# The raw weights' third buffer in the first trunk, and two re-ordered steps of the normalised operands

## The chip, the cores and the metric

The kernel runs on one core of a Trainium2 chip. The metric is the device time of one execution in microseconds (us). The core has five engines with queues of their own: TensorE (PE in the profile, with PEld for its weight loads), VectorE (DVE), ScalarE (ACT), GpSimd (POOL) and SyncE (SP). SyncE computes nothing here; it issues DMA transfers. GpSimd issues some as well.

## The reference

One layer of an encoder is applied to 1024 prompt rows and 32 sample rows (`x`), which share the weights; the model width is 1024. Cut to what is computed:

```python
h = rms_norm(x, g_mix)
q, k, v, ch, cb, cc, ga, gb = split(h @ w_in)            # 1024 x 6656
a = window_attention(q, k, v, sink) @ w_attn_out
conv = short_convolution(cc * ch, conv_w)                # width 3, causal
bo = (cb * conv) @ w_conv_out
x = x + (sigmoid(ga) * a + sigmoid(gb) * bo) @ w_mix_out
hc = rms_norm(x, g_cross)
x = x + softmax_attention(hc @ w_cq, mem_k, mem_v) @ w_co  # 256 memory tokens
hm = rms_norm(x, g_mlp)
x = x + square(relu(hm @ w_up)) @ w_down                 # 1024 -> 4096 -> 1024
y = rms_norm(x, g_final)
```

New rows of the K/V and convolution caches are outputs too. All is float32.

## The kernel before

**Layout.** Activations are held transposed: 128 features on the partitions, tokens along the free axis. The 1056 tokens are cut into three chunks `CH` of 384, 384 and 288 columns (chunks 0, 1, 2) for the first part of the layer, and into two halves for the MLP. `f` counts the eight blocks of 128 features. Each float32 operand is split into a high and a low part in TensorE's `fp32r` form, and each product is three matmuls: high by high, high by low, low by high (`gemm`, L193 to L195; `product`, L864 to L866, in the gates and the up projection; L1770 to L1772 in the down projection).

**Weights.** A weight tile of 128 x 1024 floats (512 KB) is loaded raw by SyncE (`fetch_w`, L155), then split: `wh` by an ACT cast (L129), `wl` by a DVE subtraction (L130). `next_w` keeps two split weights in stock ahead of the one in use. A raw tile is one of the two `wr` buffers of pool `wp`. While the dictionary `third` is filled, every third raw tile instead comes from the pool `third["pool"]`, under the tag `ws` (the trace calls it `wr` as well, the order `wr3`). For the keys in `kept` the low part is stored once into `wl_d` (L172) and loaded in later uses (L166) instead of being subtracted again.

**GpSimd's sums.** The MLP's products use sums of weight blocks. `sum_step` (L702 to L725) makes them on GpSimd, one piece after another: it loads raw blocks into a tile, `ws` of pool `W["pool"]` and `xacc` by turns, adds (L719), and stores the sums into `gsum_d`, `usum_d` or `wsum_d` by GpSimd's own queue (L723). One `ws` tile is all that pool has.

**Stages, in the order of the plan.** Keys and values; attention; the gates (`gate_pair`), which use a third raw buffer from a pool of theirs; then `after_gates`, which gives `third` the pool `W["pool"]` from then on. Then come the *trunks*: for each chunk eight `do_conv_out` (L1042) and eight `do_mix` (L1057). Chunk 0's trunk, with one conv_out of chunk 1 put in, runs first; chunk 1's runs beside cross attention of chunk 0; chunk 2's is made into *fillers*, 48 items together with the first up projections. After filler `i` the steps that `then(i, ...)` names are called: statistics, cross attention, and `normed(c, f)` (L1277), which makes block `f` of chunk `c` of the MLP's normalised operand: a DVE multiplication (L1279), a store into `xn_d` by SyncE (L1282), and for chunk 0 an ACT cast and a DVE subtraction (L1291). The first half's operand is made straight from chunk 0. The second half's (tiles `Z` of `xa[1]`) starts in chunk 0 and ends in chunk 1: `open_first` loads its first part back from `xn_d` (L1229) after filler 18, and `normed` of chunk 1 copies the rest from the tile `ct` (L1284). Both are SyncE's transfers. `ct` tiles come from a pool of six (`tmp`).

**What sets the order.** The plan's items are recorded in program order; a scheduler then orders each engine's instructions by its own estimate of when they can run. Instructions given to `pin` keep their place in program order relative to one another. An instruction whose semaphore is not yet reached holds all that stands behind it on its engine's queue, SyncE's transfers included.

Of the kernel before, what the change touches and what calls it, by code (L numbers as in the profile page):

```python
# [10 lines left out]
F32 = mybir.dt.float32  # L11
# [11 lines left out]
CH = [(0, 384), (384, 384), (768, 288)]  # L23
NF = 8
HT = 528
QT = 264
# [14 lines left out]
def hybrid_step(ctx: ExitStack, tc: tile.TileContext, io):  # L41
    nc = tc.nc
    act, dve, pool_e, pe, sp = nc.scalar, nc.vector, nc.gpsimd, nc.tensor, nc.sync
# [3 lines left out]
    def nm(s):  # L47
        uid[0] += 1
        return f"{s}_{uid[0]}"

    def opened(name, **kw):
        cm = tc.tile_pool(name=name, **kw)
        return cm, cm.__enter__()

    def closed(cm):
        cm.__exit__(None, None, None)
# [17 lines left out]
    def col(j):  # L74
        return prm[:, j : j + 1]
# [6 lines left out]
    xn_d = dram.tile([P, NF, NT], F32, name="xn_d")  # L82
# [14 lines left out]
    def pin(ins):  # L97
        return tc.keep_in_program_order(ins)
# [6 lines left out]
    def tmp(n, dt=F32):  # L105
        return tp.tile([P, n], dt, tag="ct", bufs=NCT, name=nm("ct"))
# [9 lines left out]
    plan, worder, kept = [], [], {}  # L116

    def item(fn, *keys):
        plan.append((fn, keys))
        worder.extend(keys)  # L120
# [11 lines left out]
    def weight(key):  # L132
        name, *at = key
        if name in ("w_down", "w_sum"):
            q, j, t = at
            return (wsum_d if name == "w_sum" else io[name])[j, t, :, :, q].rearrange("i p c -> p i c")
        if name == "g_sum":
            return gsum_d[at[0]][:, at[1]].rearrange("p h c -> p (h c)")
        src = io[name]
        for j in at:  # L140
            src = src[j]
        return src

    fetched = []
    third = {}

    def fetch_w():
        if third:
            third["n"] += 1
        if third and third["n"] % 3 == 0:  # L150
            raw = third["pool"].tile([P, 4, 256], F32, tag="ws", name=nm("wr3")).rearrange("p q c -> p (q c)")
        else:
            raw = wp.tile([P, 1024], F32, tag="wr", bufs=2, name=nm("wr"))
        src = weight(worder[wpos[0] + len(fetched)])
        sp.dma_start(raw.rearrange("p (i c) -> p i c", i=4) if len(src.shape) == 3 else raw, src)  # L155
        fetched.append(raw)

    def issue_w():
# [55 lines left out]
    def xacc_tile():  # L214
        xacc[0] = tp.tile([P, 1056], F32, tag="xacc", name=nm("xacc"))
        return xacc[0]
# [59 lines left out]
    W = {}  # L276
# [458 lines left out]
    for i, h in enumerate(hosts):  # L735
        kv, p = i // 8, i % 8
# [30 lines left out]
    def yslot(c):  # L767
        return slot(Y[c if c < 2 else "top"], f"Y{c}", CH[c][1])
# [22 lines left out]
    def pump(n):  # L791
        for into, at, t, get in coming:
            hi, lo = into[at] = (get(), get())
            pin(act.copy(hi, t))
            pin(dve.tensor_sub(lo, t, hi.bitcast(F32)))
        coming.clear()
        for into, at, src, cols, get in wanted[:n]:
            t = cols() if callable(cols) else tmp(cols)
            sp.dma_start(t, src)
            coming.append((into, at, t, get))  # L800
        del wanted[:n]
# [216 lines left out]
    def after_gates():  # L1018
        nonlocal m_cm, mpool, cr_cm, cr
        assert not pieces and "new" not in W  # L1020
        closed(x_cm)
        xacc_tile()
        third.update(n=0, pool=W["pool"])
        m_cm, mpool = opened("mpool", bufs=18, reuse_waits="tile")
        cr_cm, cr = opened("cross", bufs=1, reuse_waits="tile", side="right")

    item(after_gates)


# [191 lines left out]
    def open_first():  # L1221

        closed(m_cm)
        S["l"] = ctx.enter_context(tc.tile_pool(name="first", bufs=4, reuse_waits="tile"))
        S["z"] = ctx.enter_context(tc.tile_pool(name="second", bufs=8, reuse_waits="tile"))
        for f in range(NF):
            z = zslot()
            xa[1][f] = (quarter(z, 0), quarter(z, 1))
            sp.dma_start(xa[1][f][1].bitcast(F32)[:, : CH[0][1] - QT], xn_d[:, f, QT : CH[0][1]])  # L1229
        for name in ("w_cq", "w_co"):  # L1230
            del kept[name, 1]

# [26 lines left out]
    def zslot(dt=F32R):  # L1259
        return S["z"].tile([P, HT], dt, tag="Z", name=nm("Z"))  # L1260
# [14 lines left out]
    xa = [[None] * NF for _ in range(2)]  # L1275

    def normed(c, f):  # L1277
        t = tmp(CH[c][1])
        pin(dve.scalar_tensor_tensor(t, x1[c][f], col(G_MLP + f), R[c], op0=ALU.mult, op1=ALU.mult))  # L1279
        o, n = CH[c]  # L1280
        if c < 2 or f > 3:
            sp.dma_start(xn_d[:, f, o : o + n], t)  # L1282
        if c == 1:
            sp.dma_start(xa[1][f][1].bitcast(F32)[:, CH[0][1] - QT :], t[:, : HT - CH[1][0]])  # L1284
        if c == 2:
            top[f] = t
        if c == 0:
            hi, lo = (yslot(0)[:, :QT] for _ in range(2))
            xa[0][f] = (hi, lo)
            act.copy(hi, t[:, :QT])  # L1290
            pin(dve.tensor_sub(lo, t[:, :QT], hi.bitcast(F32)))  # L1291
# [308 lines left out]
    def cross_units(c):  # L1600
        units = [Cross(c, h) for h in ([0, 1, 2, 3] if c < 2 else [4, 0, 1, 2, 3])]
        nu = len(units)
        for i in range(nu + 2):
            calls = []
            if i < nu:
                calls.append(units[i].scores)
            if 0 <= i - 2 < nu:
                calls.append(units[i - 2].values)
            if 0 <= i - 1 < nu:
                calls.append(units[i - 1].turn)  # L1610
            yield ("call", calls)

    def cross_steps(c):

        steps = [("call", [mem_load if c == 0 else mem_load_s])]
        steps.append(("call", [lambda: chunk_stats(c)]))
        steps.append(("items", [(do_cq(c, j), ("w_cq", j)) for j in range(2)]))
        for i, step in enumerate(cross_units(c)):
            steps.append(step)
            if i < 4 - c:  # L1620
                steps.append(("call", []))
        if c:
            steps.append(("call", []))
        steps.append(("items", [(do_co(c, 0), ("w_co", 0))]))
        steps.append(("items", [(do_co(c, 1), ("w_co", 1))]))
        if c == 0:
            steps.append(("call", [lambda: chunk_stats(c)]))
        return steps

    def beside(steps, fillers, late=()):  # L1630
        for i, filler in enumerate(fillers):
            item(*filler)
            for x in [x for at, x in late if at == i]:
                item(lambda x=x: x())
            if steps:
                kind, what = steps.pop(0)
                for x in what:
                    if kind == "items":
                        item(*x)
                    else:  # L1640
                        item(lambda x=x: x())
        return steps

    def trunk(c):
        return [(do_conv_out(c, f), ("w_conv_out", f)) for f in range(NF)] + [
            (do_mix(c, f), ("w_mix", f)) for f in range(NF)
        ]

    for name, n in (("w_conv_out", NF), ("w_mix", NF), ("w_cq", 2), ("w_co", 2)):
        kept.update(((name, j), None) for j in range(1, n, 2))  # L1650

    trunks = [trunk(c) for c in range(3)]
    trunks[0].insert(NF, trunks[1].pop(0))
    left = beside([], trunks[0], [(i, lambda: pump(2)) for i in range(NF)])
    item(lambda: pump(0))
    left = beside(cross_steps(0), trunks[1])

    normeds = lambda c, at: [(at + f, lambda f=f: normed(c, f)) for f in range(NF)]
    NQ = 7
    ones_q = [up_one(i, q) for q in range(2) for i in range(NQ)]  # L1660
# [10 lines left out]
    def then(i, *what):  # L1671
        at.setdefault(i, []).extend(what)

    call = lambda fn, *args: lambda: item(lambda: fn(*args))
# [2 lines left out]
    then(1, call(chunk_stats, 1))  # L1677
    then(2, *[lambda j=j: item(do_cq(1, j), ("w_cq", j)) for j in range(2)])
    for f in range(NF):
        then(2 + f, call(normed, 0, f))  # L1680
    for i, (_, calls) in zip((3, 5, 7, 9, 11, 12), cross_units(1)):
        then(i, *[call(x) for x in calls])
    then(14, lambda: item(do_co(1, 0), ("w_co", 0)))
# [2 lines left out]
    then(17, call(chunk_row, 1))  # L1686
    assert opened_at == 18
    then(18, call(open_first))
    for f in range(NF):
        then(19 + f // 4, call(normed, 1, f))  # L1690
        then(22, call(second_split, f))
# [293 lines left out]
```

## Time and profile before

| | |
|---|---|
| median of 3 runs | 1779.99 us (1779.09 to 1783.26) |
| profiled execution, its own time | 1778.09 us |
| its span in the profile | 1776.3 us |
| PE busy | 1734.2 us, 98% |
| DVE, ACT, POOL busy | 1184.4, 852.8, 576.8 us |
| read from HBM, written | 252.82 MB, 94.19 MB |
| 512 KB loads of raw weights from the inputs, as far as the page lists them | in_w_in 53, in_w_up 53, in_w_conv_out 24, in_w_mix 24, in_w_down 24 |

The profile is of one execution. A busy time counts an engine's work without waits. Stretches are given in microseconds from the span's start; the gates end near 800, the first trunk lies behind that, the fillers from about 985 on. The clock is the share of full speed that the throttle granted TensorE. A row of waits names the instruction that waited, what ended the wait, and then the total, the count and the longest.

### The profile page before, as it was taken

How to read it: one execution, taken by the hardware profiler on the slowest of the kernel's cores; microseconds unless marked ns; L12 is line 12 of the kernel's file. 1: busy time of each engine (PE TensorE's matmuls, PEld its weight loads, DVE VectorE, ACT ScalarE, POOL GpSimd, SP SyncE). 2: the span in 40 equal slices, each digit the busy share in tenths (PEclk: the TensorE clock that was granted, in tenths of full speed). 3: DMA queues.
4: the chain of work that ended last, by engine and by line, in shares of the span. 5: the costliest groups of instructions: out<-in, count | busy, mean ns of one | idle time of the engine just before them, and what ended most of it. 6: DMA issues, size and time to landing. Idle time of an engine off the chain costs nothing.

```text
span 1776.3 us, 32569 instructions
## 1 busy us (share of the span) xinstructions
PE 1734.2 (98%) x12250; PEld 1716.3 (97%) x12250; DVE 1184.4 (67%) x2270; ACT 852.8 (48%) x1660; POOL 576.8 (32%) x651
## 2 busy tenths in 40 slices
PE   8999999999999999979999999999999999999998
PEld 8999999999999999979999989999999999999998
DVE  7776867868666647536667677786666686556575
ACT  8643534435335324324556665774444463333443
POOL 0025366543453444531225130004555510000121
PEclk9999999999999999989999998999999999999999
DMA  5333334333446888747765667575666686554554
GB/s 183 109 117 128 111 128 155 120 139 136 148 155 223 298 274 288 264 166 272 261 213 196 236 224 233 183 257 196 223 221 224 213 310 212 186 184 167 193 173 157
DMA packets 182221, 349.75 MB, mean 197 GB/s; under 512 B 19744, under 2 KB 102976, under 8 KB 181936
## 3 DMA queue, kind: packets, MB, share of 16 engines
q1 hardware_dynamic: 167008, 295.07, 49.1%
q0 software_dynamic: 15056, 52.60, 8.4%
q8 instruction: 96, 1.57, 0.4%
q14 instruction: 61, 0.50, 0.1%
HBM read 252.82 MB, written 94.19 MB: 195 GB/s over the span
## 4 chain that ended last, share of the span: by engine, by line
PE 77%; DMA 11%; POOL 6%; DVE 2%; issue 2%; ACT 2%; SPq 0%; DVEq 0%; POOLq 0%; ACTq 0%
PE acc L193 10%; PE acc L195 10%; PE acc L194 10%; PE acc L1772 6%; PE acc L1770 6%; PE acc L1771 6%; PE acc L864 5%; PE acc L866 5%; PE acc L865 5%; DMA wsum_d<-ws 3%; DMA wsum_d<-xacc 3%; POOL ws L719 2%; POOL xacc L719 2%; PE pc L864 2%; PE pc L865 2%
## 5 line engine op out<-in xcount | busy, mean ns | idle before, releaser
L129 ACT CAST wh<-wr 128x1024 fp32r<-128x1024 f32 x226 | 237.2, 1050 | 424.5 <-PE acc L1771 126.2
L130 DVE TENSOR_TENSOR wl<-wr,wh 128x1024 fp32r<-128x1024 f32 x226 | 292.5, 1294 | 140.6 <-ACT wh L129 138.6
L193 PE MATMUL acc<-X,wh 128*128 128x384 f32 (+1 forms) x864 | 281.8, 326 | 6.6 <-ACT wh L129 6.6
L194 PE MATMUL acc<-X,wh 128*128 128x384 f32 (+1 forms) x864 | 279.1, 323 | 0.0
L195 PE MATMUL acc<-X,wl 128*128 128x384 f32 (+1 forms) x864 | 278.5, 322 | 0.3 <-DVE wl L130 0.3
L269 POOL TENSOR_TENSOR xacc<-xacc,ct 128x384 f32<-128x384 f32 (+1 forms) x56 | 73.4, 1314 | 401.8 <-ACT ct L267 400.3
L193 PEld LDWEIGHTS acc<-X,wh 128*128 128x128 f32 x864 | 163.0, 189 | 7.2 <-ACT wh L129 6.6
L194 PEld LDWEIGHTS acc<-X,wh 128*128 128x128 f32 x864 | 163.1, 189 | 0.7
L195 PEld LDWEIGHTS acc<-X,wl 128*128 128x128 f32 x864 | 162.8, 188 | 0.9 <-DVE wl L130 0.8
L195 PE MATMUL acc<-Y,wl 128*128 128x384 f32 (+1 forms) x432 | 139.1, 323 | 1.8 <-DMA wl<-wl_d 1.8
L193 PE MATMUL acc<-Y,wh 128*128 128x384 f32 (+1 forms) x432 | 138.8, 323 | 0.4 <-ACT Y L774 0.4
L194 PE MATMUL acc<-Y,wh 128*128 128x384 f32 (+1 forms) x432 | 139.1, 322 | 0.0
L1770 PE MATMUL acc<-n,wh 128*128 128x264 f32 x352 | 100.2, 285 | 0.0
L1771 PE MATMUL acc<-n,wh 128*128 128x264 f32 x352 | 100.1, 284 | 0.0
L1772 PE MATMUL acc<-n,wl 128*128 128x264 f32 x352 | 100.0, 285 | 0.1
L129 ACT CAST PTh<-pt 128x512 fp32r<-128x512 f32 (+3 forms) x94 | 46.0, 516 | 111.6 <-PE pt L582 110.8
L719 POOL TENSOR_TENSOR ws<-ws 128x256 f32<-128x256 f32 x100 | 91.9, 919 | 5.6
L719 POOL TENSOR_TENSOR xacc<-xacc 128x256 f32<-128x256 f32 x100 | 87.9, 879 | 5.5 <-DMA xacc<-in_w_in 0.2
L195 PEld LDWEIGHTS acc<-Y,wl 128*128 128x128 f32 x432 | 81.1, 188 | 2.1 <-DMA wl<-wl_d 2.1
L193 PEld LDWEIGHTS acc<-Y,wh 128*128 128x128 f32 x432 | 80.9, 188 | 0.7 <-ACT Y L774 0.7
L194 PEld LDWEIGHTS acc<-Y,wh 128*128 128x128 f32 x432 | 81.1, 188 | 0.0
L864 PE MATMUL acc<-n,wh 128*128 128x264 f32 x256 | 72.9, 285 | 0.8 <-DVE Z L1502 0.8
(422 smaller groups left out, 5511.5 us busy)
## 6 DMA issues: line engine op xcount, KB each, us to landing
wr<-in_w_in SPq DMA_DIRECT2D x53, 512.0 KB, 3.7
wr<-in_w_up SPq DMA_DIRECT2D x53, 512.0 KB, 4.5
wr<-wsum_d SPq DMA_DIRECT2D x40, 512.0 KB, 3.4
wr<-in_w_conv_out SPq DMA_DIRECT2D x24, 512.0 KB, 4.3
wr<-in_w_mix SPq DMA_DIRECT2D x24, 512.0 KB, 4.8
wr<-in_w_down SPq DMA_DIRECT2D x24, 512.0 KB, 3.4
wl<-wl_d SPq DMA_DIRECT2D x18, 512.0 KB, 4.6
n_d<-Z SPq DMA_DIRECT2D x32, 264.0 KB, 4.3
```

Of the source, the lines that this page charges most:

```text
L129: act.copy(hi, src)
L130: dve.tensor_sub(lo, src, hi.bitcast(F32))
L193: pe.matmul(out, wh[:, a], hi, start=(k == 0), stop=False)
L194: pe.matmul(out, wh[:, a], lo, start=False, stop=False)
L195: pe.matmul(out, wl[:, a], hi, start=False, stop=(k == len(acts) - 1))
L719: pin(pool_e.tensor_tensor(t[:, to], t[:, x], t[:, y], op=ALU.add))
L864: pe.matmul(acc, wh[:, a], hi, start=(start and k == 0), stop=False, skip_group_check=True)
L865: pe.matmul(acc, wh[:, a], lo, start=False, stop=False, skip_group_check=True)
L866: pe.matmul(acc, wl[:, a], hi, start=False, stop=(k == 3), skip_group_check=True)
L1770: pe.matmul(a, wh[:, s], hi, start=(t == 0 and k == 0), stop=False, skip_group_check=True)
L1771: pe.matmul(a, wh[:, s], lo, start=False, stop=False, skip_group_check=True)
L1772: pe.matmul(a, wl[:, s], hi, start=False, stop=(t == 1 and k == 7), skip_group_check=True)
```

## The change

It has five parts. The third raw buffer is not given to `third` at the end of the gates but after item 12 of chunk 0's trunk (among its mixes). The first load that uses it (the third weight fetched after that) is pinned in program order. The low part of conv_out's weight 5 is no longer kept: it is subtracted again in each of its three uses. `normed(0, f)` is called after filler `f // 2` instead of `2 + f`. And the sixteen loads of the second half's operand go by GpSimd's queue instead of SyncE's.

```diff
@@ fetch_w
-        sp.dma_start(raw.rearrange("p (i c) -> p i c", i=4) if len(src.shape) == 3 else raw, src)
+        load = sp.dma_start(raw.rearrange("p (i c) -> p i c", i=4) if len(src.shape) == 3 else raw, src)
+        if third and third["n"] == 3 and third["pool"] is W["pool"]:
+            pin(load)
@@ after_gates
-        third.update(n=0, pool=W["pool"])
@@ open_first
-            sp.dma_start(xa[1][f][1].bitcast(F32)[:, : CH[0][1] - QT], xn_d[:, f, QT : CH[0][1]])
+            pool_e.dma_start(xa[1][f][1].bitcast(F32)[:, : CH[0][1] - QT], xn_d[:, f, QT : CH[0][1]])
@@ normed
-            sp.dma_start(xa[1][f][1].bitcast(F32)[:, CH[0][1] - QT :], t[:, : HT - CH[1][0]])
+            pool_e.dma_start(xa[1][f][1].bitcast(F32)[:, CH[0][1] - QT :], t[:, : HT - CH[1][0]])
@@ the plan
-        kept.update(((name, j), None) for j in range(1, n, 2))
+        kept.update(((name, j), None) for j in range(1, n, 2) if (name, j) != ("w_conv_out", 5))
...
-    left = beside([], trunks[0], [(i, lambda: pump(2)) for i in range(NF)])
+    left = beside(
+        [], trunks[0], [(i, lambda: pump(2)) for i in range(NF)] + [(12, lambda: third.update(n=0, pool=W["pool"]))]
+    )
...
-        then(2 + f, call(normed, 0, f))
+        then(f // 2, call(normed, 0, f))
```

Lines of the changed kernel stand two to three further down than those of before.

Three places show how instructions move. The first is SyncE's queue at the end of the gate stage. `wr` and `wr3` are raw weight tiles, `in_w_in` is the gates' weight and `gsum_d` a sum for the gates, `m1_d` and `a_d` hold attention results. Before:

```order
L928 DMA ct_1511_8899<-a_d2_109 128x288
L155 DMA wr3_1518_8922<-in_w_in 128x1024
L155 DMA wr3_1614_9467<-in_w_conv_out 128x1024
L155 DMA wr_1524_8974<-in_w_in 128x1024
L920 DMA m1_d1_93<-ct_1500_8837 128x384
L155 DMA wr_1532_9042<-gsum_d_106 128x1024
```

and after:

```order
L930 DMA ct_1511_8899<-a_d2_109 128x288
L155 DMA wr3_1518_8922<-in_w_in 128x1024
L155 DMA wr_1524_8974<-in_w_in 128x1024
L922 DMA m1_d1_93<-ct_1500_8837 128x384
L155 DMA wr_1532_9042<-gsum_d_106 128x1024
```

The load of a conv_out weight into a `wr3` tile has left this place. The first load into a tile of `W["pool"]` now stands near the end of chunk 0's mixes, among the first weights of chunk 1's conv_outs (SyncE, after):

```order
L155 DMA wr_1757_10065<-in_w_conv_out 128x1024
L1062 DMA ct_1742_9987<-in_x0 128x384
L155 DMA wr3_1748_10023<-in_w_conv_out 128x1024
L174 DMA wl_d_1741_9985<-wl_1740_9982 128x1024
L155 DMA wr_1766_10107<-in_w_conv_out 128x1024
```

Here it stands behind the load of a later weight (10065 is recorded after 10023).

The second place is SyncE's queue where `normed` of chunk 1 runs. `ct` holds the block, `xn_d` is its store, `Z` the second half's operand, `b11_d` and `s1_d` are stores of the up projection. Before:

```order
L1282 DMA xn_d_95<-ct_2355_12582 128x384
L1284 DMA Z_2327_12463<-ct_2355_12582 128x144
L1282 DMA xn_d_95<-ct_2356_12586 128x384
L1284 DMA Z_2328_12465<-ct_2356_12586 128x144
L1282 DMA xn_d_95<-ct_2357_12590 128x384
L1284 DMA Z_2329_12467<-ct_2357_12590 128x144
L1310 DMA b11_d_96<-lt_2353_12550 128x264
L1310 DMA s1_d_103<-lt_2367_12617 128x264
L1310 DMA b11_d_96<-lt_2368_12618 128x264
L155 DMA wr_2383_12740<-in_w_up 128x1024
```

and after:

```order
L1283 DMA xn_d_95<-ct_2338_12514 128x384
L1283 DMA xn_d_95<-ct_2339_12518 128x384
L155 DMA wr3_2375_12683<-in_w_up 128x1024
L1311 DMA s1_d_103<-lt_2366_12615 128x264
L155 DMA wr_2382_12738<-in_w_up 128x1024
L1311 DMA b11_d_96<-lt_2352_12548 128x264
L1283 DMA xn_d_95<-ct_2353_12576 128x384
L1283 DMA xn_d_95<-ct_2354_12580 128x384
L155 DMA wr_2389_12777<-in_w_up 128x1024
```

The `Z` loads are gone from this queue, and loads of `in_w_up` stand between the stores.

The third place is GpSimd's queue in the same fillers, where before only additions of squares stood (`xacc`, L269). After:

```order
L271 TENSOR_TENSOR xacc_1571_9304<-xacc_1571_9304,ct_2307_12386 128x288
L1230 DMA Z_2321_12451<-xn_d_95 128x120
...
L1230 DMA Z_2328_12465<-xn_d_95 128x120
L271 TENSOR_TENSOR xacc_1571_9304<-xacc_1571_9304,ct_2320_12441 128x288
L1285 DMA Z_2321_12451<-ct_2336_12506 128x144
L1285 DMA Z_2322_12453<-ct_2337_12510 128x144
...
L1285 DMA Z_2328_12465<-ct_2356_12588 128x144
```

One addition of a square now stands between the eight loads from `xn_d` and the eight from `ct`.

## The prediction

> **What bounds the kernel now.** I read the busy times first, then a table of stretches of the span, then the waits of PE in the stretches where it stands idle, and last the queue that feeds it there.
>
> ```profile
> span 1776.3 us, 32569 instructions
> ...
> PE 1734.2 (98%) x12250; PEld 1716.3 (97%) x12250; DVE 1184.4 (67%) x2270; ACT 852.8 (48%) x1660; POOL 576.8 (32%) x651
> ```
>
> PE is the bound: it is busy in 1734.2 of 1776.3 us, so waits of PE can give back at most 42.1 us, and beside them what it loses at a reduced clock. The change takes no matmul away. So the question is where these microseconds lie. The table of stretches (columns: stretch and its length, busy time and count of PE, PEld, DVE, ACT, POOL, then the clock granted to PE, the share of the DMA engines, GB/s) shows it:
>
> ```profile
> 720.00:780.00 60.00, 56.33 (x352) 56.01 (x350) 25.23 (x33) 15.89 (x24) 34.09 (x42) 0.99 0.56 190
> 780.00:785.00 5.00, 0.00 (x0) 0.00 (x0) 0.00 (x0) 0.39 (x1) 0.00 (x0) 0.50 0.97 327
> 785.00:790.00 5.00, 4.30 (x13) 4.18 (x14) 4.32 (x7) 4.18 (x7) 0.00 (x0) 0.50 1.03 361
> 790.00:795.00 5.00, 5.00 (x30) 5.00 (x30) 1.40 (x2) 0.85 (x2) 0.00 (x0) 0.81 0.73 236
> 800.00:860.00 60.00, 60.00 (x352) 60.00 (x351) 38.70 (x63) 28.05 (x50) 10.17 (x8) 1.00 0.77 264
> ...
> 985.00:995.00 10.00, 10.00 (x65) 10.00 (x64) 4.12 (x12) 4.28 (x10) 2.68 (x2) 1.00 0.48 177
> 995.00:1015.00 20.00, 19.56 (x149) 19.32 (x148) 16.87 (x35) 15.32 (x34) 2.85 (x3) 1.00 0.74 262
> 1015.00:1040.00 25.00, 21.35 (x147) 19.30 (x147) 22.41 (x46) 16.72 (x41) 3.77 (x5) 1.00 0.57 194
> 1040.00:1065.00 25.00, 24.58 (x173) 23.52 (x172) 16.42 (x26) 15.06 (x22) 12.07 (x12) 1.00 0.74 259
> 1065.00:1070.00 5.00, 5.00 (x28) 5.00 (x28) 1.28 (x6) 1.11 (x2) 0.21 (x1) 0.66 0.40 135
> 1070.00:1090.00 20.00, 20.00 (x162) 20.00 (x161) 17.23 (x34) 12.16 (x27) 3.30 (x3) 1.00 0.70 230
> 1090.00:1095.00 5.00, 3.56 (x25) 2.94 (x23) 3.62 (x11) 1.23 (x4) 0.00 (x0) 1.00 0.88 261
> 1095.00:1105.00 10.00, 8.48 (x47) 8.49 (x48) 7.56 (x13) 6.65 (x11) 0.00 (x0) 0.66 0.68 245
> ```
>
> Three places matter. The first is one long stop at 776 to 785, followed by matmuls at half clock. The second is a loose chain of small gaps from 995 to 1065 while DVE is nearly full (22.41 of 25 us). The third is a stop at 1091 to 1096, again with a low clock behind it. The waits of PE from 780 to 860 hold one line (total, times, longest), and SyncE's queue (start, duration, what) with one row of the chain that ended last say who made it:
>
> ```profile
> PE acc L864 <- ACT wh L129: 9.4, 1, 9.4
> ```
>
> ```profile
> 752.34 0.33 SPq L155 DMA_DIRECT2D wr<-in_w_in  x1
> 778.99 0.33 SPq L155 DMA_DIRECT2D wr<-in_w_conv_out  x1
> 779.42 0.38 SPq L155 DMA_DIRECT2D wr<-in_w_in  x1
> ```
>
> ```profile
> 775.77 3.10 DMA usum_d<-ws
> ```
>
> SyncE issues nothing for 26 us. At its head stands a load of conv_out's sixth weight into a `ws` tile, the buffer in which GpSimd still builds weight sums, and that tile is free only when the last usum_d store has landed at 778.87. The gate stage's own next weight (in_w_in, 779.42) is queued behind it, and so are two gsum_d loads. PE lives on its two weights in stock and runs dry at 776.3.
>
> **The change part by part.** *First, the third buffer.* The order shows conv_out's load gone from that place in SyncE's queue; the in_w_in load that follows waits only for a DVE step that frees its own `wr` tile. What ends there is idle time of 3.67 + 5.00 + 0.70 = 9.37 us, and work at low clock: 4.30 x 0.50 + 5.00 x 0.19 = 3.10 us. Behind the stop nothing else is late: GpSimd's chain of sums runs to 778.87 as before, and its next reader is the first mix, long after. I take -12.5 us in full; the bounds are -9.4, if the clock falls for another reason, and 0, if another load stands there.
>
> The Trainium skill (TensorE: Matmul & The Clock Gate, Part 1) says that PE drops to half clock after about 3.4 us without work, in windows that run freely. At the 9.37 us stop the trace agrees, but it also shows 0.66 at 1065 to 1070 behind gaps that make 0.42 us in all from 1040 to 1065, so short gaps cost clock here as well. By the rule alone the low clock after the third place would not be counted as gain, and the sum below would be about 2 us smaller.
>
> *What the third buffer leaves behind.* From 779 to the middle of the first mixes all weights now share the two `wr` buffers, some 13 loads. The cost depends on how fast two buffers turn:
>
> ```profile
> wr<-in_w_conv_out SPq DMA_DIRECT2D x24, 512.0 KB, 4.3
> ```
>
> ```profile
> L129 ACT CAST wh<-wr 128x1024 fp32r<-128x1024 f32 x226 | 237.2, 1050 | 424.5 <-PE acc L1771 126.2
> L130 DVE TENSOR_TENSOR wl<-wr,wh 128x1024 fp32r<-128x1024 f32 x226 | 292.5, 1294 | 140.6 <-ACT wh L129 138.6
> ```
>
> ```profile
> ACT wh L129 <- DMA wr<-in_w_conv_out: 5.5, 2, 3.3
> ```
>
> A buffer is taken for 4.3 us of load, 1.05 of ACT and 1.29 of DVE, 6.6 us, so two buffers give a weight each 3.3 us. PE eats one in 24 matmuls (eight blocks of 128 rows, three products each), and 352 matmuls took 60 us (800 to 860), so 4.1 us each. That leaves 2 x (4.1 - 3.3) = 1.6 us per load for waiting in SyncE's queue, and two ready weights (8.2 us) as stock. In the stretch before, loads came late to ACT twice already, 5.5 us in all, with the third buffer present and PE not waiting. So the cover is thin. I take +2 us, bounds 0 (the cover holds) and +5 (5.5 us of lateness once more, now uncovered); it sits nearer 0 because PE stood nowhere from 800 to 860.
>
> *conv_out's weight 5 is no longer kept.* One store and two loads of 512 KB less, two DVE subtractions of 1.29 us more. DVE has room (38.70 of 60 us), the transfers are beside other work: 0.
>
> *Second, the normed operands of chunk 0, eight steps brought from fillers 2 to 9 up to 0 to 3.* Each issues two DVE steps, one ACT cast and one store in SyncE's queue.
>
> ```profile
> 998.93 0.62 DVE L1279 SCALAR_TENSOR_TENSOR ct<-Ga,prm,R 128x384 f32<-128x384 f32 x1
> ...
> 1006.96 0.43 DVE L1291 TENSOR_TENSOR Y<-ct,Y 128x264 fp32r<-128x264 f32 x1
> ```
>
> That is 1.05 us of DVE each. Steps 4 to 7 ran in 1015 to 1040, so 4.2 of 22.41 us leave the stretch in which PE lost 3.65 us; 985 to 995 has 5.9 us of DVE free to take the first ones. At stake are the gaps 0.44 + 3.65 + 0.42 = 4.5 us and 5 x 0.34 = 1.7 us of clock, 6.2 in all. Against it: each step now takes two of the six `ct` tiles per filler until SyncE's store has gone, beside the conv_out products that need a `ct` tile to empty their accumulator, and 995 to 1015 was already at 16.87 of 20 us on DVE. I take -2.5, with bounds -6.2 and +4 (one more gap like the 3.65, earlier).
>
> *Third, sixteen loads of the second half from SyncE's queue to GpSimd's.*
>
> ```profile
> 1078.47 0.44 SPq L1282 DMA_DIRECT2D xn_d<-ct  x1
> ...
> 1088.73 0.47 SPq L1284 DMA_DIRECT2D Z<-ct  x1
> ...
> 1090.86 0.94 SPq L155 DMA_DIRECT2D wr<-in_w_up  x2
> ```
>
> ```profile
> 1095.14 1.04 ACT L129 CAST wh<-wr 128x1024 fp32r<-128x1024 f32 x1 [3.23 <-DMA wr<-in_w_up]
> ```
>
> ```profile
> 1096.52 0.59 PE L864 MATMUL acc<-Z,wh 128*128 128x264 f32 x1 [2.27 <-ACT lt L1324]
> ```
>
> Between 1078.47 and 1089.2 SyncE issues nothing but the sixteen xn_d and Z transfers, each pair held by its DVE step. The w_up loads come at 1090.86, ACT waits for them until 1095.14, and PE's 2.27 us are named for ACT's copy behind that cast. In the new order w_up loads stand between the stores. At stake: 1.44 + 1.52 = 2.96 us idle and 8.48 x 0.34 = 2.88 us of clock, 5.8 in all. What is late next are the Z operands themselves:
>
> ```profile
> 1090.64 0.41 ACT L1296 CAST Z<-Z 128x264 fp32r<-128x264 f32 x1 [0.23 <-DMA Z<-ct]
> ```
>
> ```profile
> 775.05 1.45 POOL L723 DMA_DIRECT2D usum_d<-ws  x2 [0.41 <-POOL ws L719]
> ...
> 1150.91 1.68 POOL L269 TENSOR_TENSOR xacc<-xacc,ct 128x288 f32<-128x288 f32 x2 [75.01 <-ACT ct L267]
> ```
>
> GpSimd issues a transfer in 1.45 / 2 = 0.73 us, and is idle for 75 us from 1076 on. Eight loads of xn_d cost it 5.8 us, and one addition stands behind them: chunk 2's last square, which the statistics (L224) wait for; PE now meets those 56 rows later in its order. Eight Z loads then follow one DVE step each. In before the last Z load was issued at 1088.73 by SyncE, and the ACT cast that reads it began at 1090.64, 1.9 us later; with a GpSimd issue and a landing of the same length it comes at about the same time. I take -4, with bounds -5.8 and +2 (three late issues of 0.73).
>
> The Trainium skill (DMA: Bandwidth & Descriptors, SWDGE vs HWDGE vs iDMA) speaks against this edit: GpSimd writes its descriptors into on-chip memory and DVE can lock it out of that in some modes, while SyncE's transfers are immune. No row of this trace shows GpSimd issuing beside a DVE as full as 17.23 of 20 us. By the rule the Z operands would be late, the edit would give nothing, and the sum would be 4 us smaller.
>
> **Sum.** -12.5 + 2 + 0 - 2.5 - 4 = -17.0 us against the profiled execution, which took 1778.09 us (its span 1776.3 and 1.8 around it): 1761.1. The median of the runs before is 1779.99, 1.9 above that, so I forecast 1763.
>
> **The rivals.** *Some of it is handed back (1771).* The long stop goes, but the gains of the second and third edits don't come (+6.5) and the two buffers cost their +5 instead of +2, or part of it: -17 + 6.5 + 2 = -8.5. For it: thin cover at the loads, `ct` tiles, a full DVE. Against it: the order has the w_up loads between the stores.
>
> *All of it comes (1756).* Both later places close (-6.2 and -5.8) and two buffers suffice: -24.5. For it: the causes are named in the trace. Against it: DVE is near full whatever the order.
>
> *The stop moves (1779).* Another load held by GpSimd's sums stands at SyncE's head. This would be the case that the change doesn't do what it says. The third buffer's first load now stands near the end of the first mixes, some 90 us after the sums have landed, and the gsum_d loads wait for stores that are long done; little speaks for it.
>
> *Slower (1787): two buffers starve PE from 800 to 870.* Without my +2 the sum is -19, and these 19 us must be lost over 13 weights after a stock of 8.2 us: (19 + 8.2) / 13 = 2.1 us per weight, that is a turn of 2 x (4.1 + 2.1) = 12.4 us instead of 6.6. It decides from 12.4 - 6.6 = 5.8 us of hold per load in SyncE's queue, behind tiles that DVE and GpSimd free. At 6.8 us the turn is 13.4, the stretch costs (6.7 - 4.1) x 13 - 8.2 = 26 us against 19, and the time is 1787. For it: DMA at 0.77 and loads late twice. Against it: those two were 5.5 us together, not each.
>
> **How the numbers follow.** About 0.3%, 5.3 us, is what a measurement of this kernel can tell from no change. Chances: the forecast 0.60 (1758 to 1768), all of it 0.12, handed back 0.14 (of which 0.01 within the 5.3 us), the stop moves 0.05, slower 0.09. Faster is 0.60 + 0.12 + 0.13 = 0.85, same 0.01 + 0.05 = 0.06, slower 0.09. The lowest sum of the bounds is -12.5 + 0 - 6.2 - 5.8 = -24.5, 1755.5; the range begins at 1754. To the other side it reaches through the handed-back case to 1775; left out are the last two rivals and the end of that case, about 0.16.
>
> **What would show it.** In the profile after, SyncE issues in_w_in within some us of 753, no wait of over 2 us stands at 776, and the clock there is 1.00. PE stays near 60 of 60 us in the first trunk, DVE falls below 22 of 25 us in the stretch that was 1015 to 1040, and w_up loads stand between the xn_d stores. I am wrong if ACT's waits for `wr` from conv_out pass 10 us, if PE waits at the first Z product for over 3 us, or if a wait of SyncE for a `ws` tile comes back elsewhere.

## The result, and the profile after

The changed kernel took 1757.92 us (median of 4 runs, 1753.62 to 1762.53), the kernel before, run beside it, 1780.03 us: a ratio of 0.9873, 95% interval 0.9839 to 0.9907. That is 22 us faster, where 17 were forecast, and inside the range, which begins at 1754. A second set of runs of the same program gave 1760.39 us against 1778.86, ratio 0.9896 (0.9878 to 0.9914), so 18.5 us. The profiled execution took 1762.53 us with a span of 1760.8, 15.5 less than the span before.

The page's head, and the table of stretches of the kernel after (columns as before: stretch, length, then busy time and count of PE, PEld, DVE, ACT, POOL, then clock, DMA share, GB/s):

```profile
span 1760.8 us, 32586 instructions
...
PE 1726.3 (98%) x12250; PEld 1710.8 (97%) x12250; DVE 1189.4 (68%) x2272; ACT 853.7 (48%) x1660; POOL 585.0 (33%) x667
```

```profile
720.00:780.00 60.00, 60.00 (x375) 60.00 (x374) 31.34 (x41) 21.43 (x33) 35.55 (x43) 1.00 0.73 249
780.00:785.00 5.00, 5.00 (x36) 5.00 (x35) 0.98 (x2) 0.48 (x1) 0.36 (x1) 1.00 0.65 227
785.00:790.00 5.00, 5.00 (x32) 5.00 (x31) 2.89 (x5) 1.77 (x3) 0.00 (x0) 1.00 0.17 41
...
800.00:860.00 60.00, 57.86 (x331) 57.22 (x330) 38.85 (x62) 29.12 (x53) 10.85 (x9) 1.00 0.78 262
860.00:880.00 20.00, 17.37 (x90) 16.74 (x89) 10.53 (x14) 10.15 (x16) 6.01 (x5) 0.91 0.84 293
880.00:900.00 20.00, 20.00 (x118) 20.00 (x118) 12.49 (x24) 10.75 (x18) 5.27 (x4) 1.00 0.52 184
...
980.00:1000.00 20.00, 18.51 (x127) 17.87 (x126) 18.04 (x36) 12.41 (x23) 2.45 (x3) 1.00 0.59 192
1000.00:1020.00 20.00, 18.14 (x128) 17.91 (x128) 16.42 (x37) 13.69 (x35) 3.67 (x5) 0.91 0.64 217
1020.00:1040.00 20.00, 20.00 (x152) 19.98 (x151) 16.97 (x31) 14.93 (x31) 8.27 (x8) 1.00 0.71 230
...
1080.00:1100.00 20.00, 18.68 (x139) 17.31 (x138) 16.98 (x38) 12.84 (x27) 1.07 (x2) 1.00 0.69 239
```

PE's idle time fell from 42.1 to 34.5 us and its busy time, for the same 12250 matmuls, from 1734.2 to 1726.3. Busy time multiplied by the missing share of the clock, added up over rows of 5 us, is 11.2 us before and 4.7 after, so most of that difference is time at a lower clock. The long stop is gone: PE is busy through all of 720 to 790 at a clock of 1.00. SyncE's queue (start, duration, what) shows why: the row below holds two loads of in_w_in, and both have been issued by 757.18. In the kernel before the second of them left only at 779.42. GpSimd's sums no longer hold it up, though their last store is issued at 778.91.

```profile
754.09 3.09 SPq L155 DMA_DIRECT2D wr<-in_w_in  x2
```

Two things are new. In 800 to 880 PE now loses 2.14 + 2.63 = 4.8 us; its two longest waits there, of 1.6 and 2.4 us, are for DVE's emptying of a conv_out accumulator and for a stored low part. And the crowd on DVE has moved from 1015 to 1040 (22.41 of 25 us before) to 980 to 1000 (18.04 of 20).

### The profile page after: what moved, and what is told of

Its sections match the earlier page's. It is cut to its first block, busy times and chain, and to the rows that moved or that the text cites. A ratio compares the mean times of both kernels' runs of the same rounds, so it can differ in the third digit from the quotient of the medians.

```text
span 1760.8 us, 32586 instructions
## 1 busy us (share of the span) xinstructions
PE 1726.3 (98%) x12250; PEld 1710.8 (97%) x12250; DVE 1189.4 (68%) x2272; ACT 853.7 (48%) x1660; POOL 585.0 (33%) x667
## 4 chain that ended last, share of the span: by engine, by line
PE 52%; DMA 4%; DVE 2%; ACT 2%; POOL 1%; issue 1%; DVEq 0%; SPq 0%; POOLq 0%; ACTq 0%
PE acc L1773 6%; PE acc L1774 6%; PE acc L1775 6%; PE acc L866 5%; PE acc L867 5%; PE acc L868 5%; PE acc L195 3%; PE acc L197 2%; PE acc L196 2%; PE pc L867 2%; PE pc L868 2%; PE pc L866 2%; DMA ct<-m_d 1%; DMA ct<-in_x 1%; PE pa L196 1%
## 5 line engine op out<-in xcount | busy, mean ns | idle before, releaser
L129 ACT CAST wh<-wr 128x1024 fp32r<-128x1024 f32 x228 | 239.4, 1050 | 419.6 <-PE acc L1774 128.6
L1774 PE MATMUL acc<-n,wh 128*128 128x264 f32 x352 | 100.2, 285 | 0.0
L1773 PE MATMUL acc<-n,wh 128*128 128x264 f32 x352 | 100.2, 285 | 0.0
L570 ACT ACTIVATE S<-S,nmx 128x257 f32<-128x257 f32 (+1 forms) x132 | 64.2, 488 | 20.7 <-DVE nmx L565 19.4
```

The source lines that it names most:

```text
L129: act.copy(hi, src)
L1773: pe.matmul(a, wh[:, s], hi, start=(t == 0 and k == 0), stop=False, skip_group_check=True)
L1774: pe.matmul(a, wh[:, s], lo, start=False, stop=False, skip_group_check=True)
```

## The experiments

All edits are against the changed kernel. "Gain" is the distance of a kernel's median to the median of before run beside it; where an edit of the change is undone, what is missing from the 18.5 us of the changed kernel's second set is what that edit carries.

| kernel | median us | gain us | ratio (95%) |
|---|---|---|---|
| again (changed kernel) | 1760.39 | 18.5 | 0.9896 (0.9878 to 0.9914) |
| nopin | 1770.83 | 8.0 | 0.9953 (0.9938 to 0.9969) |
| no_third | 1762.86 | 16.0 | 0.9906 (0.9886 to 0.9926) |
| pin_only | 1769.21 | 9.3 | 0.9951 (0.9938 to 0.9964) |
| late | 1765.58 | 14.3 | 0.9925 (0.9912 to 0.9939) |
| no_norm | 1765.99 | 12.9 | 0.9936 (0.9913 to 0.996) |
| no_pool | 1766.30 | 12.2 | 0.9937 (0.9922 to 0.9951) |
| only_third | 1774.07 | 5.8 | 0.9958 (0.9942 to 0.9974) |
| sp1 | 1761.53 | 18.3 | 0.9899 (0.9886 to 0.9912) |
| norm_1f2 | 1765.09 | 13.4 | 0.9934 (0.9918 to 0.9949) |
| keep5 | 1759.18 | 19.3 | 0.9896 (0.9882 to 0.991) |
| drop1 | 1764.33 | 15.5 | 0.9913 (0.99 to 0.9926) |

### The changed kernel once more (again)

> The changed kernel once more, unaltered. Its four executions so far lie in two groups, 1753.6 and 1754.5, 1761.3 and 1762.5 us, and the only profile is of the later group. Theory G: the groups are the kernel's own (which gaps of TensorE pull its clock down), and both come back, 1753 to 1755 and 1761 to 1763, with the clock as the difference. Theory D: it was a drift of one session, and all runs lie within 4 us.

All four values lie from 1759.5 to 1761.5. Theory G fell: the two groups did not come back. Theory D (all within 4 us) fits this set. What made the first set spread over 9 us stays open, so all comparisons below start from this second set.

### What took the stop away: nopin, no_third, pin_only

The diff removes two things from the place of the stop at once: the early hand-over of the third buffer, and the scheduler's freedom to put its first load early. Three kernels take them apart.

```diff
 nopin
-        if third and third["n"] == 3 and third["pool"] is W["pool"]:
-            pin(load)
 no_third (after_gates; the late hand-over goes)
+        third.update(n=0, pool=W["pool"])
 pin_only: no_third, and also
-            pool_e.dma_start(...)   # twice
+            sp.dma_start(...)
-        then(f // 2, call(normed, 0, f))
+        then(2 + f, call(normed, 0, f))
 (and weight 5 kept)
```

> The changed kernel without the pin of the first load into the shared tile; the later hand-over of the third buffer stays. In the order of SyncE this load then stands where it stood before, ahead of the gates' in_w_in load. Theory P (the pin takes the stop away): the stop at 776 comes back, 9 us idle and 3 us of clock, so 12.5 us slower than the changed kernel, about 1770. Theory L (the later hand-over takes it away): no stop, the same time as the changed kernel within 3 us.

> The changed kernel with the third buffer handed over at the end of the gates again, as before; the pin stays. Theory P: no stop at 776, and the stretch from 800 to 900 has three buffers again, so it is 2 to 5 us faster than the changed kernel, about 1754. Theory L: the stop comes back, about 1770. If two buffers cost nothing, the time is that of the changed kernel, 1758.

> The kernel before with nothing but the pin of the first load into the shared tile; the third buffer is handed over at the end of the gates as before. Theory P (the pin alone takes the stop away): the stop at 776 is gone, 10 to 13 us faster than before, 1766 to 1769. Rival: without the other edits the time moves to the places of before and less than 8 us remain, over 1771.

Without the pin 10.4 us of the gain are lost, and the stop is back although the buffer is handed over later. The waits of PE from 760 to 800 in nopin (what waited, what ended it, then total, count, longest), and SyncE's queue:

```profile
PE acc L864 <- ACT wh L129: 8.6, 1, 8.6
```

```profile
753.58 0.33 SPq L155 DMA_DIRECT2D wr<-in_w_in  x1
779.12 0.33 SPq L155 DMA_DIRECT2D wr<-in_w_conv_out  x1
779.55 0.38 SPq L155 DMA_DIRECT2D wr<-in_w_in  x1
```

The load at 779.12 is now the weight of a much later item, chunk 1's second conv_out, and the scheduler has drawn it forward to the same place. The order shows it in SyncE's queue of nopin, ahead of the gates' own load:

```order
L155 DMA wr3_1518_8922<-in_w_in 128x1024
L155 DMA wr3_1748_10023<-in_w_conv_out 128x1024
L155 DMA wr_1524_8974<-in_w_in 128x1024
```

So theory L fell and theory P holds in its main point: the pin alone ends the stop, and pin_only, which has it and nothing else of the change, gains 9.3 us (10 to 13 were expected). Three prices of the stop lie near each other: in nopin's profile 8.6 us of idle time and, with 3.83 us of matmuls at a clock of 0.50 from 785 to 790, 1.9 us of clock; 10.4 us by undoing the pin; 9.3 us by the pin alone. The last is a net gain: from 800 to 900, 980 to 1070 and 1070 to 1110 PE idles 3.4, 5.3 and 5.0 us in pin_only's profile, where before had 2.7, 4.5 and 3.0.

What the later hand-over is for shows in no_third. The stop stays away there too, but the 2 to 5 us that theory P expected from a third buffer did not come. Pinned, the load may not stand ahead of what was recorded before it, but it can end up behind what was recorded later. In no_third it is conv_out's sixth weight, placed behind the loads of the next two, and PE waits for it near 821 (waits of PE, 800 to 860; below it ACT's cast that the wait is for):

```profile
PE acc L195 <- ACT wh L129: 2.1, 2, 1.8
```

```profile
820.33 2.00 ACT L129 CAST wh<-wr 128x1024 fp32r<-128x1024 f32 x2 [2.16 <-DMA wr<-in_w_conv_out]
```

With hand-over after item 12 that wait is not there. The median moved by 2.5 us, but the intervals of no_third and again overlap, and with both later edits undone the sign turns (pin_only gains 9.3, only_third, with the late hand-over and without weight 5, 5.8). The hand-over's own worth is not settled; it is small beside the pin's.

### Whether two buffers starve PE: late

```diff
-        ... + [(12, lambda: third.update(n=0, pool=W["pool"]))]
     left = beside(cross_steps(0), trunks[1])
+    item(lambda: third.update(n=0, pool=W["pool"]))
```

> The changed kernel with the third buffer handed over only after chunk 1's trunk, so that some 20 weights more run on two buffers. Theory: two buffers feed TensorE (in the profiles no wait for a raw weight or its high part stands from 790 to 870), so no such wait appears in chunk 1's trunk either and the time is within 2 us of 1760. Rival (the prediction's +2 per 13 loads): 3 us slower, about 1763, with waits for wh after 880.

By the medians it lost 4.2 us of the gain, near what the rival gave (the intervals of late and again just touch), but not in the rival's way. Before 980 no wait of PE is for a raw weight or its high part, so both trunks ran on two buffers without one; then comes a single stop, in the waits of PE from 880 to 1000, and SyncE's queue names it:

```profile
PE acc L195 <- ACT wh L169: 6.7, 1, 6.7
```

```profile
976.66 0.32 SPq L1283 DMA_DIRECT2D xn_d<-ct  x1
...
978.10 3.25 SPq L1283 DMA_DIRECT2D xn_d<-ct  x2
981.47 0.37 SPq L1047 DMA_DIRECT2D ct<-m_d  x1
982.48 0.32 SPq L1283 DMA_DIRECT2D xn_d<-ct  x1
983.10 0.33 SPq L155 DMA_DIRECT2D wr<-in_w_cq  x1
```

The pinned first load is now in_w_cq (a weight of cross attention). It stands behind four stores of normed blocks, the last of which goes out right after its DVE step, and it leaves at 983.10, when PE has been standing since 980.98. So two buffers do feed PE through both trunks, which is the theory's point, and the longest stop is at the place at which the pinned load lands.

### The two later edits: no_norm, no_pool, only_third

```diff
 no_norm, only_third
-        then(f // 2, call(normed, 0, f))
+        then(2 + f, call(normed, 0, f))
 no_pool, only_third
-            pool_e.dma_start(xa[1][f][1]...)   # both lines
+            sp.dma_start(xa[1][f][1]...)
```

> The changed kernel with the normed steps of chunk 0 back at fillers 2 to 9. Theory N (the prediction's): the gaps of 1015 to 1040 come back, 2.5 us slower, about 1760. Rival: the changed kernel's trace names DVE's emptying of conv_out accumulators for four waits of TensorE, 5.0 us in all, three of them in the fillers where the steps now stand; if the steps only moved the crowding, the time is the same within 2 us or 1 to 3 us faster.

> The changed kernel with the sixteen loads of the second half back on SyncE's queue. Theory Q (the prediction's): the w_up loads come late again, TensorE stands 2 to 3 us at the first Z products with a low clock behind it, 4 us slower than the changed kernel, 1762 to 1766. Rival: the earlier normed steps alone cleared that place; the same time within 1.5 us.

> The changed kernel with both later edits undone: normed steps at fillers 2 to 9 and the sixteen loads on SyncE's queue; pin, later hand-over and weight 5 as in the change. Undone one at a time these two cost 5.6 and 5.9 us against the changed kernel's 1760.4. Theory A (two separate places, so they add): 1771 to 1773. Theory B (each works only with the other, since what one leaves late meets the other's place): 1765 to 1768, no slower than undoing one.

By the medians the first is worth 5.6 us, the second 6.3, and both together 12.7. So theory N and theory Q hold in their direction, with sizes above the 2.5 and 4 us expected, and both rivals fell; the interval of no_norm just touches that of again, that of no_pool does not. That the two add (theory A) is likely but not settled: the six executions of only_third lie in two groups, 1768 to 1769 and 1774 to 1776, its interval overlaps those of no_norm and no_pool, and by the differences of the ratios the losses are 7.1, 7.3 and 11.0 us. The stretches 980 to 1070 (fillers) and 1070 to 1110 (first Z products) of again, no_norm, no_pool and only_third, in that order, show two separate places:

```profile
980.00:1070.00 90.00, 87.03 (x635) 85.99 (x634) 74.45 (x135) 58.69 (x116) 32.06 (x36) 0.98 0.67 222
1070.00:1110.00 40.00, 38.47 (x286) 36.65 (x285) 32.09 (x69) 23.29 (x52) 2.15 (x4) 0.96 0.74 242
```

```profile
980.00:1070.00 90.00, 82.95 (x596) 80.68 (x595) 71.41 (x131) 57.52 (x114) 26.20 (x31) 0.98 0.63 207
1070.00:1110.00 40.00, 38.84 (x291) 37.47 (x291) 33.37 (x67) 23.90 (x54) 4.31 (x8) 0.96 0.76 259
```

```profile
980.00:1070.00 90.00, 86.02 (x635) 84.66 (x634) 74.79 (x144) 59.26 (x118) 25.40 (x24) 1.00 0.67 221
1070.00:1110.00 40.00, 32.62 (x241) 31.84 (x240) 27.54 (x55) 21.89 (x44) 0.00 (x0) 0.91 0.71 231
```

```profile
980.00:1070.00 90.00, 81.64 (x544) 78.89 (x543) 65.76 (x125) 53.89 (x110) 20.83 (x22) 0.92 0.57 189
1070.00:1110.00 40.00, 35.96 (x279) 35.52 (x278) 32.81 (x65) 22.25 (x42) 1.22 (x2) 0.96 0.82 260
```

PE's idle time in the first stretch is 3.0 us with the early normed steps (again) and 7.1 without; with the Z loads on SyncE 4.0 and 8.4. In the second stretch it is 1.5 with GpSimd's queue and 7.4 without; with late normed steps 1.2 and 4.0. In no_pool PE's longest wait there is 5.6 us, for a load of in_w_cq that is issued at 1076.58, right behind the last of the stores and copies; in before the late loads were those of in_w_up. The idle time that each edit takes away in its own stretch, 4.1 us (7.1 less 3.0) and 5.9 us (7.4 less 1.5), is of the size of what the medians lose. In only_third a lower clock comes on top in the first stretch, 0.92 against 0.98.

### Which of the sixteen loads, and where the normed steps stand: sp1, norm_1f2

```diff
 sp1 (open_first only)
-            pool_e.dma_start(..., xn_d[:, f, QT : CH[0][1]])
+            sp.dma_start(..., xn_d[:, f, QT : CH[0][1]])
 norm_1f2
-        then(f // 2, call(normed, 0, f))
+        then(1 + f // 2, call(normed, 0, f))
```

> The changed kernel with the eight loads from xn_d back on SyncE's queue; the eight copies from ct stay on GpSimd's. Theory C (the copies from ct hold the queue, each behind its DVE step; the loads from xn_d wait for nothing then): the same time as the changed kernel within 1.5 us, 1759 to 1762. Rival: sixteen issues less is what counts, so half of the 5.9 us comes back, 1763.

> The changed kernel with the normed steps of chunk 0 called after filler 1 + f // 2, one filler later than in the change. Theory W (two steps per filler crowd DVE beside the emptying of conv_out accumulators, wherever they stand): the same three waits for DVE, 3 us in all, the same time within 2 us. Theory V (it is the meeting with the statistics of chunk 1 in the first filler): the waits fall below 1.5 us and it is 2 us faster.

In sp1 nothing is lost (0.2 us): the eight loads from `xn_d`, issued in one run, did not matter, and the eight copies from `ct` carry all of it. The time is the one that theory C gave and the rival fell. Its reason, that each copy is held by its DVE step, does not fit the queue's rows; that is taken up below, under GpSimd's queue.

In norm_1f2 both theories fell. One filler later costs 5 us, nearly as much as undoing the edit. The three largest of PE's waits from 980 to 1070 are now the following. In again the first is 3.0 us in the same stretch and the other two do not occur; there the only other wait is one of 0.7 us for statistics:

```profile
PE acc L195 <- DVE ct L1051: 4.2, 3, 2.7
PE o L1177 <- ACT PTh L129: 1.4, 1, 1.4
PE acc L195 <- DVE Gb L1066: 1.0, 1, 1.0
```

PE now also waits in cross attention (L1177), besides the emptying of accumulators. Which of the meetings decides was not tried; that one filler more or less changes the time is shown.

### The kept low parts: keep5, drop1

```diff
 keep5
-        ... for j in range(1, n, 2) if (name, j) != ("w_conv_out", 5))
+        ... for j in range(1, n, 2))
 drop1
+        ... if (name, j) not in (("w_conv_out", 1), ("w_conv_out", 5)))
```

> The changed kernel, but the low part of conv_out's weight 5 is kept again (one store and two loads of 512 KB more, two DVE subtractions less). The prediction's cost of this edit is 0: the same time within 2 us, 1758 to 1762. Rival: TensorE's wait for a low part loaded late (2.0 to 2.5 us at 876) gets longer or doubles, 2 to 4 us slower.

> The changed kernel, with the low part of conv_out's weight 1 no longer kept either. In the profiles of the changed kernel TensorE waits 2.0 to 2.45 us at 876 for the load of that low part, which took 7.1 us among three loads of raw weights. Theory: the wait goes and with it some clock, 2 to 3.5 us faster than the changed kernel, 1757 to 1758. Rival: the subtraction that replaces it stands behind the same raw loads and the wait is only renamed; the same time within 1 us.

keep5 is the same time within the intervals, as the prediction's 0 had it, and its rival fell. In drop1 the theory fell: the wait for the stored low part did go (of PE's waits from 786 to 1070, those for a subtraction are 0.8 us in all), but the time is not shorter. By the median 3 us are lost; the intervals of drop1 and again overlap. The largest waits of the same view are now:

```profile
PE acc L195 <- DVE ct L1051: 2.2, 2, 1.5
PE o L1177 <- ACT PTh L129: 1.4, 1, 1.4
PE pr L243 <- ACT ct L241: 1.1, 1, 1.1
```

The last two are new against again. The first is smaller than there:

```profile
PE acc L195 <- DVE ct L1051: 4.1, 4, 1.4
```

So waits went and others came, and PE's idle time in the whole span is nearly that of again (32.5 us against 31.9). Neither theory had this, and where 3 us would have gone is not shown. No run beat the changed kernel clearly: keep5 is 0.9 us ahead of it in gain, at the same ratio.

## Why the prediction was right, step by step

**The bound and the long stop: right; the size at the upper end.** Twelve and a half us were counted from the rows of before; the runs put it at 9.3 to 10.4, with 8.6 + 1.9 = 10.5 in nopin's profile, where the low clock is over by 790. Since the 9.3 is net of other idle time that came, the size stays open between 9.3 and 12.5. The step was right that the stop ends and that nothing stands behind it. It was incomplete in its cause: it read the load's disappearance from SyncE's order and gave it to the moved third buffer as a whole. The pin did it. The move alone leaves the stop where it was, with another load at SyncE's head, which is what the rival "the stop moves" feared: that is nopin, at 1771 with the other edits' gain.

**Two buffers, +2: about right in size, wrong in cause.** The stretch 800 to 880 lost 4.8 us of idle time against 1.0 before in the same window, but no wait of PE in it is for a raw weight. The rows of before are:

```profile
860.00:880.00 20.00, 19.03 (x108) 18.25 (x107) 13.51 (x18) 10.93 (x20) 4.44 (x4) 1.00 0.70 239
880.00:900.00 20.00, 18.23 (x107) 17.91 (x107) 9.83 (x19) 9.78 (x18) 6.04 (x5) 1.00 0.79 281
```

Raw weights did come later to ACT; its waits from 795 to 880, of which before had only 5.5 us for conv_out, are now these:

```profile
ACT wh L129 <- DMA wr<-in_w_mix: 6.5, 3, 4.5
ACT wh L129 <- DMA wr<-in_w_conv_out: 5.9, 2, 3.8
ACT wh L169 <- DMA wr<-in_w_conv_out: 3.4, 1, 3.4
```

That is 15.8 us, of which 9.3 are for conv_out, just under the 10 that the prediction named as a sign of being wrong. No wait of PE follows from it, so the weights in stock covered all of it; late went on like this for a whole trunk more. The sign "PE stays near 60 of 60 us" failed by a little: it is 57.86. What PE waited for were DVE's emptying (1.6 us) and the stored low part (2.4 us, 1.8 before, then at 885). PE did not starve, as the slower rival had it. Part of the loss is only moved, since the low part's wait of before fell just behind 880: from 800 to 900 PE idles 2.7 us before, 4.8 in the first profile after and 3.1 in again. So the idle cost is 0.4 to 2.1 us, with 1.3 us of low clock beside it in the first of these two profiles only. How much of it two buffers cause is not shown; no_third, which has the third buffer, idles 2.5 us there.

**Weight 5, 0: right** (keep5).

**The normed steps, -2.5: right in sign, too small.** Undone, they cost 5.6 us by the medians, near the outer bound of 6.2. The step counted the gaps of the kernel before, 4.5 us and their clock. With the rest of the change in place the same steps late cost 7.1 us of idle time in the fillers, not 4.5: the place had become tighter than the profile of before showed. Why, no run shows. The feared crowding at the new place came too: three waits for DVE, 3.0 us, in again.

**GpSimd's queue, -4: right in sign, too small, and wrong in what holds the queue.** Undone it costs 6.3 us by the medians. The step said that each pair of transfers is held by its DVE step. The same queue says otherwise when all its durations are added: from the first at 1078.47 to the end of the last at 1089.20 are 10.7 us, and the sixteen issues themselves, of 0.44 to 0.86 us, make up 8.7 of these. The DVE steps were done before: the last two ended at 1085.13 and 1086.86, and their stores left at 1086.97 and 1088.13. DVE even waited once for a transfer, which had to free a `ct` tile (before):

```profile
1084.51 0.62 DVE L1279 SCALAR_TENSOR_TENSOR ct<-Gb,prm,R 128x384 f32<-128x384 f32 x1 [1.21 <-DMA Z<-ct]
```

So SyncE was mostly not waiting, it was issuing. With that it fits that half as many transfers help, and that sp1's eight loads do no harm: they leave in one run of 3.65 us right behind a w_up load, and the next load of a weight goes out 3.7 us after the run's end. GpSimd's price was counted at 0.73 us an issue and is lower (its timeline after):

```profile
1063.03 4.31 POOL L1230 DMA_DIRECT2D Z<-xn_d  x8
1067.36 0.83 POOL L271 TENSOR_TENSOR xacc<-xacc,ct 128x288 f32<-128x288 f32 x1
1069.42 2.41 POOL L1285 DMA_DIRECT2D Z<-ct  x4 [1.24 <-DVE ct L1280]
```

Eight issues in 4.31 us are 0.54 each, with DVE busy for 16.72 of the 20 us around them. Of the rule of the Trainium skill (DMA: Bandwidth & Descriptors, SWDGE vs HWDGE vs iDMA) that was weighed against this edit no effect is seen here. It speaks of some modes of DVE only, and no row shows whether DVE was in one of them.

**The sum.** -10 for the pin, about -6 for each of the later edits, and 0.4 to 2 us on the other side from 800 to 900, make about -20 to -21.5, between the 18.5 and the 22 us that were measured. The forecast of 17 was close partly by luck: by the medians the stop's end gave 2 to 3 us less than was counted, and that offset part of two edits counted too small. The first set's 1757.92 lies just below the case called the forecast (1758 to 1768), in the one called "all of it comes"; the second set's 1760.39 lies in the forecast.

## What to carry to other kernels

Where a scheduler places loads by its own estimate, look in the order for a load whose buffer another engine still holds: here it blocked the queue for 26 us for everyone behind it, and handing the buffer over later did not end that. Pinning that one load did; but a pinned load can then sit behind loads recorded later, so choose the first one to be one with time to spare. And before calling a queue held up, add its own issue durations: a queue of small transfers can be full with issuing alone.

## What the runs showed of the hardware

The clock did not follow the length of PE's waits. In the profile of again the row of 1050 to 1055 granted 0.71, though the idle time of the 10 us ahead of it was 0.69 us, a single wait:

```profile
1050.00:1055.00 5.00, 5.00 (x34) 5.00 (x33) 1.90 (x6) 1.32 (x2) 0.00 (x0) 0.71 0.63 206
```

In norm_1f2 PE waited 1.4 and 0.7 us near 1001 and 1002, 0.7 us before 1007 and 2.7 us before 1015. The rows from 1000 to 1010 granted 0.81 and 0.85, but behind the longest wait the clock was full:

```profile
1015.00:1020.00 5.00, 5.00 (x37) 5.00 (x38) 4.94 (x14) 1.87 (x5) 1.77 (x2) 1.00 0.62 202
```

In that whole execution 1.2 us of clock were lost, against 11.2 in before, as the 5 us rows below 1.00 add up. In again's row 1.5 us of clock (5.00 x 0.29) stand behind 0.69 us of idle time, so little waiting can go with more loss in clock than in idle time. That the wait set the clock off is not shown; whether a low clock follows a wait of this size differs between executions of nearly the same program.
